# Attention scores whose low-part product contracts over 64 rows instead of 128, with keys copied by the vector engine instead of by transfers, and a regrouped projection and normalisation around them

## The chip, the cores and the metric

The kernel runs on one core of a Trainium2 chip. The core has a matrix engine (TensorE, PE in the profile, whose weight loads are listed apart as PEld), a vector engine (DVE), an activation engine (ACT), a general engine (POOL) and SyncE (SP), whose queue issues most transfers. The metric is the device time of one execution in microseconds (us). Before the change the median of three runs is 1168.81 us (1167.73 to 1170.11).

## The reference

Two decoder layers over 512 tokens of width 1024, in float32. Layer 0 mixes eight "a" heads (dilated sliding windows, merged by their softmax denominators) with eight "b" heads (window of 128, two key heads for eight query heads, a learned sink per head). Layer 1 has sixteen "c" heads of causal attention with a cumulative forget gate. Each layer ends in a squared-ReLU MLP of width 4096. Cut to what matters here:

```python
q = rms_norm(q.reshape(B, S, heads, 64), q_gain)      # over the 64 of a head
k = rms_norm(k.reshape(B, S, heads, 64), k_gain)
s = q @ k.T * 64 ** -0.5 + bias                        # bias: window and distance, or the forget gate
p = softmax(s)                                         # a: one sum over three windows; b: with a sink
y = p @ v
x = x + concat(y) @ w_out
x = x + square(relu(rms_norm(x) @ w_up)) @ w_down
```

## The kernel before, in words

**Arithmetic.** Float32 operands are used as two parts, a high part (the value rounded to the engine's fast float type) and a low part (value minus high part). A dense product is three matmuls: high by high, high by low, low by high (L163, L166, L167 in `mm3`; L230 to L232 in `project`). So nearly every operand is split, by a copy that makes the high part (`whi`, on ACT or POOL) and a subtraction that makes the low part (`wlo`, on DVE or POOL).

**Stages.** Start and first projection; layer 0 attention, up to about 235 us; its MLP, up to about 600 us; layer 1 attention, up to about 835 us; its MLP. In an attention stage two streams of work are woven into each other: dense matmuls (projections of the next heads, then the output projection) and the heads that are ready. `run` draws from the two generators by a ratio: `n_att` attention steps against `n_dense` units of dense work, with a lead. A step ends at each `yield`. A scheduler then orders each engine's instructions by priority, lower first, and by its own estimate of when operands are ready.

**One pair of heads.** `norm_heads` takes a projection out of four PSUM banks (copies L246), squares it (L248, ACT, out of PSUM), sums over 64 columns (L249), makes the inverse root on DVE (L252 and L127 to L133) and multiplies it in (L259: two of the four row tiles on DVE, two on POOL, by `NORM`). `prep_q` and `prep_k` transpose 128 columns, that is two heads, into a PSUM bank (`qkT`, L266). For head h, `prep_q` puts q's high part on the head's own 64 partitions (L276, ACT) and q's low part on the other 64 (L277, DVE). `prep_k` puts k's high part in block 0 and its low part in block 1 of a tile, both on the head's own 64 partitions (L158 ACT, L159 DVE), and a transfer copies both blocks to the other 64 partitions (L289, on SP's queue, 26 in all).

**Scores and softmax.** For each of four query tiles i, two matmuls make the scores (L324, L325): the stationary operand is the 128-partition column of q, high over low; the moving operand is block 0, then block 1 of k. Both contract over all 128 partitions, so that the two products carry all four part products. A "c" head adds a mask matmul (L327). A DVE instruction adds the bias and takes the row extreme (L338), ACT takes the exponential and its sum (L341), DVE the reciprocal (L344, one per tile i), and POOL (ACT for i = 3) scales the tile (L349, L346).

**Values.** For each key tile c, PE transposes the probabilities into a PSUM bank (L361); ACT and DVE split it (L373, L374); then eight matmuls per head make the output (L381), which is put together on ACT and DVE (L384, L385). The values of a head are made in the steps of the next head's scores.

Of the kernel before, what the change touches and what calls it, by code (L numbers as in the profile page):

```python
# [9 lines left out]
F32 = mybir.dt.float32  # L10
F32R = mybir.dt.float32r
# [26 lines left out]
NORM = 'vgvg'  # L38
PSC = 'ggga'
GRAIN = 4  # L40
STARTPIN = 4
# [30 lines left out]
def trunk(ctx, tc, x, g_mix, g_mlp, w_in_even, a_q_gain, a_k_gain, b_q_gain, b_k_gain, b_sinks,  # L72
# [45 lines left out]
    ecol = consts.tile([P, NT], F32, name="ecol")  # L118

# [71 lines left out]
    def layer_attention(li, hT, w_in, w_out, stats=None):  # L191


        with ExitStack() as c2:
# [9 lines left out]
            nc.gpsimd.memset(p3[:, :, 256:384].bitcast(F32), 0.0)  # L204
# [34 lines left out]
            def norm_heads(outs, nh, sq_tag="sq", sq_bufs=1 + li):  # L239
# [10 lines left out]
                v = small.tile([P, NT, 8], F32, tag="ssv", name="ssv")  # L250
                for t in range(NT):
                    nc.vector.tensor_scalar(v[:, t, :nh], ss[:, t, :nh], 1.0 / HD, ecol[:, t:t + 1],  # L252
                                            op0=OP.mult, op1=OP.add)
                rs = small.tile([P, NT, 8], F32, tag="rs", name="rs")
                rsqrt_small(rs[:, :, :nh], v[:, :, :nh])
                for t in range(NT):
                    q = qk[t // 2][:, t % 2, :w].rearrange("p (h d) -> p h d", d=HD)
                    eng = nc.gpsimd if NORM[t] == "g" else nc.vector
                    eng.tensor_mul(q, q, rs[:, t, :nh].unsqueeze(2).to_broadcast([P, nh, HD]))  # L259
                return qk  # L260
# [8 lines left out]
            def prep_q(qk, off):  # L269

                pt = head_T(qk, off)
                q = ap.tile([P, 2, 512], F32R, tag="Q", bufs=2, name="Q")
                for h in range(2):
# [3 lines left out]
                    nc.vector.tensor_sub(q[r2, h], pt[r], q[r, h].bitcast(F32))  # L277
                return q

            def prep_k(qk, off, g):  # L280
# [3 lines left out]
                for h in range(2):  # L284
                    k = ap.tile([P, 2, 512], F32R, tag="K", bufs=3, name="K")
# [15 lines left out]
            def scores(q, k, j, kind, h, pr):  # L301
# [11 lines left out]
                rden = small.tile([P, NT], F32, tag="rden", name="rden")  # L313
                for i in range(NT):
# [9 lines left out]
                    nc.tensor.matmul(s[:, :n], qs, k[:, 0, k0:k0 + n], start=True, stop=False)  # L324
                    nc.tensor.matmul(s[:, :n], qs, k[:, 1, k0:k0 + n], start=False, stop=kind != "c")  # L325
# [18 lines left out]
                    nc.vector.reciprocal(rden[:, i:i + 1], den[:, i:i + 1])  # L344
                    if PSC[i] == "a":
                        nc.scalar.activation(p[:, :nv], p[:, :nv], AF.Copy, scale=rden[:, i:i + 1])  # L346
                    else:
                        eng = nc.gpsimd if PSC[i] == "g" else nc.vector
                        eng.tensor_scalar(p[:, :nv], p[:, :nv], rden[:, i:i + 1], 1.0, op0=OP.mult, op1=OP.mult)  # L349
                    yield  # L350

            def values(pr, kind, V, vs, yf, j):

                pts = []
# [890 lines left out]
```

## Time and profile before

| what | us or share |
|---|---|
| median of three runs | 1168.81 |
| the profiled execution, its own time | 1168.43 |
| its span in the trace | 1166.7 |
| PE busy, of the span | 98% |
| DVE, ACT, POOL busy | 75%, 55%, 17% |
| layer 0 attention, from 45 to 235 us | 190 |
| layer 1 attention, from 600 to 835 us | 235 |

A page of the profile gives each engine's busy time and share. Matmuls are pipelined: each one is listed with its whole latency, so that the records of PE overlap, and what a matmul costs in a full stream is the distance from its start to the start of the next one, not its duration. A weight load (PEld) normally starts while the matmul before it still runs. "Idle before" is time of an engine without work, and the name behind it is what the profile holds for its releaser: this is inferred from the time of a semaphore event, and can be wrong.

### The profile page before, as it was taken

What the parts mean: (1) busy time and instruction counts of PE and PEld (TensorE: products, weight loads), DVE (VectorE), ACT (ScalarE), POOL (GpSimd) and SP (SyncE); (2) the same over time, 40 slices, a digit from 0 to 9 for tenths busy, and PEclk for the clock granted to TensorE, in tenths of its full rate; (3) what the DMA queues carried; (4) which work ended last, traced back from release to release, by engine and by line L of the source; (5) the groups of instructions that cost most, each with busy time, mean ns of one, the idle gap of its engine ahead of it and who ended that gap; (6) DMA issues with size and microseconds to landing.
All of it is one profiled execution on the core that took longest, in us unless ns stands there. A gap on an engine that the chain in (4) does not pass through costs nothing.

```text
span 1166.7 us, 17503 instructions
## 1 busy us (share of the span) xinstructions
PE 1146.8 (98%) x6256; PEld 982.5 (84%) x6256; DVE 880.7 (75%) x1877; ACT 647.1 (55%) x1349; POOL 202.4 (17%) x296
## 2 busy tenths in 40 slices
PE   8999989999999999999999999999999999999998
PEld 7987877888988988988887888888888888888887
DVE  7878999968858857855647877788858759669676
ACT  6555867556545545444235675656756455465452
POOL 1345444200000000000255445332100000000000
PEclk9999999999999999999999999999999999999999
DMA  7522014242333333333443333343430721623403
GB/s 253 163 76 89 19 57 146 70 126 78 104 108 91 91 108 91 106 111 110 146 128 109 107 84 109 107 118 113 163 105 4 235 87 55 198 73 109 147 33 109
DMA packets 100655, 126.57 MB, mean 108 GB/s; under 512 B 6184, under 2 KB 79944, under 8 KB 100568
## 3 DMA queue, kind: packets, MB, share of 16 engines
q1 hardware_dynamic: 99384, 121.23, 34.3%
q10 hardware_dynamic: 608, 2.13, 0.5%
q0 software_dynamic: 576, 2.10, 0.4%
q8 instruction: 49, 0.80, 0.3%
q14 instruction: 38, 0.31, 0.1%
HBM read 112.29 MB, written 6.32 MB: 102 GB/s over the span
## 4 chain that ended last, share of the span: by engine, by line
PE 85%; DVE 8%; DMA 2%; POOL 1%; issue 1%; ACT 1%; SPq 0%; ACTq 0%; POOLq 0%; DVEq 0%
PE up L163 10%; PE up L167 10%; PE up L166 10%; PE pj L230 5%; PE pj L232 5%; PE pj L231 5%; PE O L381 3%; PE PT L361 2%; PE Y L1021 2%; PE Y L1019 2%; PE Y L1022 2%; PE op L167 2%; PE op L163 2%; PE op L166 2%; PE Y L1068 1%; PE S L324 1%
## 5 line engine op out<-in xcount | busy, mean ns | idle before, releaser
L163 PE MATMUL up<-xin,whi 128*128 128x512 f32 x512 | 200.5, 392 | 0.0
L167 PE MATMUL up<-xin,whi 128*128 128x512 f32 x512 | 199.3, 389 | 0.0
L166 PE MATMUL up<-xin,wlo 128*128 128x512 f32 x512 | 199.2, 389 | 0.0
L768 ACT CAST whi<-wraw 128x512 fp32r<-128x512 f32 x228 | 139.2, 619 | 105.0 <-PE up L167 47.7
L769 DVE TENSOR_TENSOR wlo<-wraw,whi 128x512 fp32r<-128x512 f32 x228 | 151.7, 686 | 50.8 <-ACT whi L768 50.5
L167 PEld LDWEIGHTS up<-xin,whi 128*128 128x128 f32 x512 | 96.1, 188 | 20.1
L166 PEld LDWEIGHTS up<-xin,wlo 128*128 128x128 f32 x512 | 96.2, 188 | 19.8 <-issue 0.2
L163 PEld LDWEIGHTS up<-xin,whi 128*128 128x128 f32 x512 | 96.1, 188 | 19.8 <-issue 0.2
L341 ACT ACTIVATE P<-P,negm 128x128 f32<-128x128 f32 (+5 forms) x128 | 69.5, 544 | 51.7 <-DVE negm L338 47.9
L950 ACT ACTIVATE u<-up 128x512 f32<-128x512 f32 x64 | 38.3, 599 | 90.9 <-PE up L167 90.8
L230 PE MATMUL pj<-whi,hn 128*128 128x512 f32 (+2 forms) x256 | 88.7, 346 | 0.0
L232 PE MATMUL pj<-whi,hn 128*128 128x512 f32 (+2 forms) x256 | 86.9, 339 | 0.0
L231 PE MATMUL pj<-wlo,hn 128*128 128x512 f32 (+2 forms) x256 | 86.8, 339 | 0.0
L151 POOL TENSOR_SCALAR whi<-wraw 128x512 fp32r<-128x512 f32 x88 | 60.5, 689 | 143.0 <-PE pj L232 121.8
L789 DVE TENSOR_TENSOR t<-u 128x256 f32<-128x256 f32 x56 | 23.2, 424 | 62.8 <-ACT u L1093 61.0
L154 POOL TENSOR_TENSOR wlo<-wraw,whi 128x512 fp32r<-128x512 f32 x48 | 64.4, 1346 | 20.7 <-ACT whi L149 17.9
L230 PE MATMUL pj<-whi,h 128*128 128x512 f32 (+1 forms) x192 | 66.5, 353 | 0.7 <-DVE v L159 0.7
L232 PE MATMUL pj<-whi,h 128*128 128x512 f32 (+1 forms) x192 | 65.5, 343 | 0.0
L231 PE MATMUL pj<-wlo,h 128*128 128x512 f32 (+1 forms) x192 | 65.5, 341 | 0.0
L349 POOL TENSOR_SCALAR P<-P,rden 128x256 f32<-128x256 f32 (+2 forms) x96 | 47.7, 500 | 90.8 <-DVE rden L344 90.0
L154 DVE TENSOR_TENSOR wlo<-wraw,whi 128x512 fp32r<-128x512 f32 (+1 forms) x72 | 49.9, 700 | 17.7 <-POOL whi L151 14.5
L373 ACT CAST PT<-PT 128x256 fp32r<-128x256 f32 (+3 forms) x128 | 49.5, 405 | 19.4 <-PE PT L361 18.5
(229 smaller groups left out, 3054.4 us busy)
## 6 DMA issues: line engine op xcount, KB each, us to landing
wraw<-in_w_up SPq DMA_DIRECT2D x64, 512.0 KB, 3.8
wraw<-in_w_down SPq DMA_DIRECT2D x56, 512.0 KB, 4.2
wraw<-in_w_in_odd SPq DMA_DIRECT2D x36, 256.0 KB, 3.3
mraw<-in_w_down SPq DMA_DIRECT2D x16, 512.0 KB, 4.4
K<-K SPq DMA_DIRECT2D x26, 256.0 KB
wraw<-in_w_in_even SPq DMA_DIRECT2D x10, 512.0 KB, 4.0
wraw<-in_w_in_even SPq DMA_DIRECT2D x16, 256.0 KB, 4.5
xl<-xsp SPq DMA_DIRECT2D x8, 512.0 KB
```

Of the source, the lines that this page charges most:

```text
L151: nc.gpsimd.tensor_scalar(dst_h, src, 1.0, 1.0, op0=OP.mult, op1=OP.mult)
L154: in_order((nc.gpsimd if lo == "pool" else nc.vector).tensor_sub(dst_l, src, dst_h.bitcast(F32)))
L163: m = nc.tensor.matmul(o, wh, xh, start=start, stop=False, skip_group_check=more)
L166: nc.tensor.matmul(o, wl, xh, start=False, stop=False, skip_group_check=more)
L167: nc.tensor.matmul(o, wh, xl, start=False, stop=stop, skip_group_check=more)
L230: nc.tensor.matmul(o, xh, hi[:, :n], start=k == 0, stop=False)
L231: nc.tensor.matmul(o, xh, lo[:, :n], start=False, stop=False)
L232: nc.tensor.matmul(o, xl, hi[:, :n], start=False, stop=k == DC - 1)
L341: nc.scalar.activation(p[:, :ne], p[:, :ne], AF.Exp, scale=-1.0, bias=negm[:, i:i + 1], accum_out=den[:, i:i + 1])
L373: nc.scalar.copy(dst[:, 0], pt[:, :n])
L768: sca(nc.scalar.copy(dst_h, src))
L769: late.append(lambda: vec(nc.vector.tensor_sub(dst_l, src, dst_h.bitcast(F32))))
```

## The change

What it does:

- **Scores.** q's high part is now written to both halves of the partitions (one more ACT copy per head and pair), and q's low part goes to a third block, each head on its own 64 partitions. k has its high part on the head's own 64 partitions and its low part on the other 64, in one block. The first matmul contracts over 128 partitions as before. The second has q's low part as stationary operand and k's high part as moving operand, over the 64 partitions of one head only. The product of the two low parts is left out.
- **Keys.** The 26 transfers of k are gone: DVE writes the low part straight to the other half. For the "b" heads, whose keys serve query heads of both halves, two ACT copies (`KH`) put the high part there as well.
- **Projection of the "b" heads.** 256 columns (keys and values) and then 512 (queries) become 384 twice, the second time with the values.
- **Normalisation.** All four copies out of PSUM come first; squares are taken from the copy, and all that follows gets a priority lower by 100. The four small L252 instructions become one, and all four multiplications are on DVE.
- **Softmax scale.** The reciprocals of i = 0, 1, 2 are one instruction, behind i = 2.
- **Values.** Key tiles 3 and 2 share one bank and one split (for "b" heads, 0 and 1 as well): three or two splits instead of four. A head thereby has one step less ("b": two less); the ratios given to `run` stay.

```diff
             def norm_heads(outs, nh):
...
                 for t in range(NT):
-                    q = qk[t // 2][:, t % 2, :w]
-                    nc.scalar.copy(q, outs[t][:, :w])
-                    sq = ap.tile([P, 512], F32, tag=sq_tag, bufs=sq_bufs, name="sq")
-                    nc.scalar.activation(sq[:, :w], outs[t][:, :w], AF.Square)
-                    nc.vector.reduce_sum(ss[:, t, :nh], sq[:, :w].rearrange("p (h d) -> p h d", d=HD), axis=AX.X)
...
-                    eng = nc.gpsimd if NORM[t] == "g" else nc.vector
-                    eng.tensor_mul(q, q, rs[:, t, :nh].unsqueeze(2).to_broadcast([P, nh, HD]))
+                    nc.scalar.copy(qk[t // 2][:, t % 2, :w], outs[t][:, :w])
+                with later(LATER):
+                    for t in range(NT):
+                        q = qk[t // 2][:, t % 2, :w]
+                        sq = ap.tile([P, 512], F32, tag="sq", bufs=1 + li, name="sq")
+                        nc.scalar.activation(sq[:, :w], q, AF.Square)
...
+                        nc.vector.tensor_mul(q, q, rs[:, t, :nh].unsqueeze(2).to_broadcast([P, nh, HD]))
...
-                q = ap.tile([P, 2, 512], F32R, tag="Q", bufs=2, name="Q")
+                q = ap.tile([P, 3, 512], F32R, tag="Q", bufs=2, name="Q")
                 for h in range(2):
                     r = slice(h * HD, (h + 1) * HD)
                     r2 = slice((1 - h) * HD, (2 - h) * HD)
                     nc.scalar.copy(q[r, h], pt[r])
-                    nc.vector.tensor_sub(q[r2, h], pt[r], q[r, h].bitcast(F32))
+                    nc.vector.tensor_sub(q[r, 2], pt[r], q[r, h].bitcast(F32))
+                    nc.scalar.copy(q[r2, h], pt[r])
...
-                    scale_split(k[r, 0], k[r, 1], pt[r], g[r])
-                    nc.sync.dma_start(k[r2].bitcast(F32), k[r].bitcast(F32))
-                    ks.append(k)
+                    in_order(nc.scalar.activation(k[r], pt[r], AF.Copy, scale=g[r]))
+                    in_order(nc.vector.scalar_tensor_tensor(k[r2], pt[r], g[r], k[r].bitcast(F32), op0=OP.mult, op1=OP.subtract))
+                    his = [k, k]
+                    if both:
+                        his[1 - h] = ap.tile([P, 512], F32R, tag="K", bufs=4, name="KH")
+                        nc.scalar.copy(his[1 - h][r2], k[r].bitcast(F32))
+                    ks.append((k, his))
...
-                    nc.tensor.matmul(s[:, :n], qs, k[:, 0, k0:k0 + n], start=True, stop=False)
-                    nc.tensor.matmul(s[:, :n], qs, k[:, 1, k0:k0 + n], start=False, stop=kind != "c")
+                    nc.tensor.matmul(s[:, :n], qs, k[0][:, k0:k0 + n], start=True, stop=False)
+                    r = slice(j * HD, (j + 1) * HD)
+                    nc.tensor.matmul(s[:, :n], q[r, 2, i * P:(i + 1) * P], k[1][j][r, k0:k0 + n], start=False,
+                                     stop=kind != "c")
...
-                for c in range(NT):
+                for cs in (((0, 1), (3, 2)) if kind == "b" else ((0,), (1,), (3, 2))):
...
-                    return project([(2048, 2304)], use, PAT_START)
+                    return project([(1792, 2048), (2176, 2304)], use)
```

In the order of the instructions two places matter. The first is PE in layer 0, where the first pair of "a" heads gets its scores. `S<-K,Q` are the score matmuls, `pj` the dense projection woven around them. Before (L324 is the first of a pair, L325 the second):

```order
L231 MATMUL pj_615<-wlo,h_5_281 128x256
L232 MATMUL pj_615<-whi,h_5_281 128x256
L324 MATMUL S<-K,Q 128x256
L325 MATMUL S<-K,Q 128x256
L324 MATMUL S<-K,Q 128x256
L325 MATMUL S<-K,Q 128x256
L324 MATMUL S<-K,Q 128x384
L325 MATMUL S<-K,Q 128x384
```

And now (L338 is the first of a pair, L340 the second, which contracts over 64 partitions):

```order
L237 MATMUL pj_615<-whi,h_1_170 128x384
L338 MATMUL S<-K,Q 128x256
L340 MATMUL S<-K,Q 128x256
L238 MATMUL pj_615<-wlo,h_1_170 128x384
L239 MATMUL pj_615<-whi,h_1_170 128x384
L338 MATMUL S<-K,Q 128x256
L340 MATMUL S<-K,Q 128x256
L237 MATMUL pj_612<-whi,h_2_208 128x384
```

Every L340 stands between two matmuls that contract over 128 partitions, here and in all of the program (128 of them). The scores also moved forward: ten dense matmuls of 384 columns lie between the transposes of this pair and its first score, where 42 of 256 columns lay before.

The second place is ACT at the same pair: the casts that make q's and k's parts, up to the first exponential. Before:

```order
L276 CAST Q<-qkT 64x512
L158 ACTIVATE K<-qkT,gg 64x512
L276 CAST Q<-qkT 64x512
L158 ACTIVATE K<-qkT,gg 64x512
L341 ACTIVATE P,den<-P,negm 128x128
```

And now (L283 is q's high part on the own half, L285 on the other half):

```order
L283 CAST Q<-qkT 64x512
L297 ACTIVATE K<-qkT,gg 64x512
L285 CAST Q<-qkT 64x512
L283 CAST Q<-qkT 64x512
L297 ACTIVATE K<-qkT,gg 64x512
L285 CAST Q<-qkT 64x512
L357 ACTIVATE P,den<-P,negm 128x128
```

Six casts instead of four stand ahead of the exponentials, and the first score waits for the first three.

More of the change, by code (lines that the diff above doesn't have):

```diff
@@ L1 @@
-from contextlib import ExitStack
+from contextlib import ExitStack, contextmanager
 import numpy as np
@@ L343, in scores @@
                     pr.append(p)
[L344 to L349, printed above, removed]
+                    ps_.append(p[:, :nv])
@@ new lines, in scores @@
+                    if i >= 2:
+                        i0 = 0 if i == 2 else 3
+                        nc.vector.reciprocal(rden[:, i0:i + 1], den[:, i0:i + 1])
+                        for n in range(i0, i + 1):
+                            if PSC[n] == "a":
+                                nc.scalar.activation(ps_[n], ps_[n], AF.Copy, scale=rden[:, n:n + 1])
+                            else:
+                                nc.gpsimd.tensor_scalar(ps_[n], ps_[n], rden[:, n:n + 1], 1.0, op0=OP.mult, op1=OP.mult)
```

86 lines of the change are left out of this document (48 added, 38 removed).

## Prediction

> **What bounds the kernel now.** I read the page first, then the waits of PE, then the stages, then single matmuls in the timeline.
>
> ```profile
> PE 1146.8 (98%) x6256; PEld 982.5 (84%) x6256; DVE 880.7 (75%) x1877; ACT 647.1 (55%) x1349; POOL 202.4 (17%) x296
> ```
>
> And the busy times of the four attention stretches, PE first, then PEld, DVE, ACT, POOL:
>
> ```profile
> 45.00:110.00 65.00, 62.12 (x370) 53.47 (x369) 50.61 (x139) 34.15 (x87) 34.86 (x48) 1.00 0.31 90
> 110.00:160.00 50.00, 48.09 (x325) 41.84 (x324) 46.35 (x158) 39.56 (x118) 23.63 (x59) 1.00 0.13 43
> 160.00:235.00 75.00, 72.12 (x377) 59.59 (x376) 70.35 (x161) 49.42 (x115) 23.42 (x31) 1.00 0.32 93
> 600.00:835.00 235.00, 231.87 (x1371) 197.33 (x1370) 184.14 (x475) 144.02 (x335) 96.30 (x125) 1.00 0.39 111
> ```
>
> PE is the bound everywhere: it lacks 2.9, 1.9, 2.9 and 3.1 us, 10.8 us in all. Since each record of a matmul reaches past its start-to-start distance, the true loss is somewhat larger; I take up to 14 us as all that a change of waits can bring. From 110 to 235 us DVE is at 93% (46.35 of 50, 70.35 of 75), so there it is the second limit. What PE waits for, with total, times and longest:
>
> ```profile
> PE S L324 <- DMA K<-K: 2.6, 3, 1.1
> PE S L324 <- DVE yf L385: 1.8, 2, 1.6
> PE S L324 <- DVE Q L277: 1.8, 2, 1.5
> PE qkT L266 <- DVE qk L259: 1.3, 2, 0.9
> PE O L381 <- DVE PT L374: 0.8, 2, 0.6
> PE PT L361 <- DVE negm L338: 0.8, 2, 0.6
> PE pj L230 <- DVE v L159: 0.7, 1, 0.7
> ```
>
> The transfers of k cost 2.6 us of PE time, DVE in six places 7.2 us. So little can be won; what the change does to the matmuls themselves weighs more.
>
> **The matmuls.** Their number is the same, 6247 in the program. The projection moves 96 matmuls of 512 and 96 of 256 columns to 192 of 384. In a full stream they start this far apart:
>
> ```profile
> 35.01 0.39 PE L231 MATMUL pj<-wlo,h 128*128 128x512 f32 x1
> 35.24 0.39 PE L232 MATMUL pj<-whi,h 128*128 128x512 f32 x1
> ```
>
> ```profile
> 626.66 0.34 PE L325 MATMUL S<-K,Q 128*128 128x384 f32 x1
> 626.84 0.23 PE L327 MATMUL S<-maskb,identb 128*128 128x128 bf16 x1
> ```
>
> ```profile
> 640.51 0.28 PE L232 MATMUL pj<-whi,hn 128*128 128x256 f32 x1
> 640.63 1.04 PE L266 MATMUL qkT<-ident,qk 128*128 128x128 f32 x8
> 641.42 0.36 PE L230 MATMUL pj<-whi,hn 128*128 128x256 f32 x1
> 641.62 0.28 PE L231 MATMUL pj<-wlo,hn 128*128 128x256 f32 x1
> ```
>
> That is 0.23 us for 512 columns, 0.18 for 384, 0.12 for 256: 96 x (0.23 + 0.12) = 34 us against 192 x 0.18 = 35 us. Nothing within a microsecond. The last four rows are also a control: eight transposes over 128 rows plus one matmul of 256 take 640.63 to 641.62, 0.99 us, that is 8 x 0.11 + 0.12 within the rounding. Going to transposes and back costs nothing.
>
> The second score matmul is another matter: 128 times it contracts over 64 rows between matmuls that contract over 128. The trace has one such excursion in a dense stream, the transpose of 22 rows of gains right behind the matmul of 35.24 above (the number ahead of the star is the rows, the one behind it the columns of the stationary operand):
>
> ```profile
> 35.56 0.24 PE L623 MATMUL pg<-ident,rows 22*128 22x22 f32 x1
> 35.72 0.38 PE L230 MATMUL pj<-whi,h 128*128 128x256 f32 x1
> 35.95 0.28 PE L231 MATMUL pj<-wlo,h 128*128 128x256 f32 x1
> ```
>
> Its weight load and the next one, and the semaphores that its line waited for:
>
> ```profile
> 35.55 0.13 PEld L623 LDWEIGHTS pg<-ident,rows 22*128 22x128 f32 x1 [0.35 <-ACT whi L149]
> 35.72 0.19 PEld L230 LDWEIGHTS pj<-whi,h 128*128 128x128 f32 x1
> ```
>
> ```profile
> L623 PEldq EVENT_SEMAPHORE  x5: 51/51/51, 2.7 to 31.7; - x5
> ```
>
> The weight load for the 22 rows should have run beside the 512-column matmul and let the next one start at 35.24 + 0.23 = 35.47. It started at 35.55, 0.09 late, and only then loaded. The next load, of full rows, came at 35.72 instead of beside the short matmul, and the matmul on it could stream only when it was in: 35.72 to 35.95 is 0.23 where 0.12 is the rule. From 35.24 to 35.95 it took 0.71 us; with a transpose of full rows it would be 0.23 + 0.11 + 0.12 = 0.46. The excursion cost 0.25 us. The named releaser (the cast of a weight tile) is a coincidence of time: the transpose reads rows whose semaphores had been seen by 31.7 us (last line) and no weight tile. So PE empties itself when the number of rows changes, and weight loads are not hidden on either side.
>
> The Trainium skill says so of tiling modes: "TensorEngine Tiling (Array Packing)", section Key Properties, has it that a change of mode, not of the tile alone, drains the engine. By that rule every one of the 128 matmuls pays twice, as in the sum below; a reading by which a half-height matmul is just a smaller one gives nothing. The trace agrees for the 22 rows and disagrees for a narrow stationary operand, which is the second rival.
>
> For a score matmul I put the pieces together: 0.09 late, 0.11 for the load that is no longer hidden, its own 256 columns as before, then a rest of 0.02 to 0.09 (0.17 between the two loads above, less 0.11 of loading and 0.03 of streaming; or as late as at the entry), and 0.11 for the next load. That is 0.33 to 0.40; the bare figure of 0.25 is the lower bound, since the short transpose's own slot was itself a weight load's. 128 times: 32 us below, 42 by 0.33, 51 above. I take 42, the low end of the built price, since half of the exits go to the short bf16 mask load. It is all on PE, the bound, and nothing hides it.
>
> **The rest, by engine.** Prices:
>
> ```profile
> L276 ACT CAST Q<-qkT 64x512 fp32r<-64x512 f32 x32 | 18.6, 582 | 28.8 <-PE qkT L266 20.4 <-DVE Q L277 8.2
> L159 DVE SCALAR_TENSOR_TENSOR K<-qkT,gg,K 64x512 fp32r<-64x512 f32 x26 | 19.5, 749 | 0.7
> L373 ACT CAST PT<-PT 128x256 fp32r<-128x256 f32 x48 | 17.4, 371 | 11.1 <-PE PT L361 10.8
> L373 ACT CAST PT<-PT 128x384 fp32r<-128x384 f32 x24 | 11.4, 477 | 2.4 <-PE PT L361 2.3
> L373 ACT CAST PT<-PT 128x128 fp32r<-128x128 f32 x32 | 8.5, 264 | 2.3 <-PE PT L361 2.3
> L344 DVE RECIPROCAL rden<-den 128x1 f32<-128x1 f32 x128 | 19.9, 159 | 7.0 <-ACT P L341 5.2
> L252 DVE TENSOR_SCALAR ssv<-ss,ecol 128x8 f32<-128x8 f32 x28 | 9.6, 362 | 0.2
> L259 DVE TENSOR_TENSOR qk<-qk,rs x16: 294/1526/1553, 44.2 to 759.9; 128x512 f32<-128x512 f32 x14, 128x128 f32<-128x128 f32 x2
> L259 POOL TENSOR_TENSOR qk<-qk,rs x16: 443/1488/1544, 44.3 to 759.4; 128x512 f32<-128x512 f32 x14, 128x128 f32<-128x128 f32 x2
> 705.62 0.69 DVE L259 TENSOR_TENSOR qk<-qk,rs 128x512 f32<-128x512 f32 x1
> 54.71 3.34 DMA K<-K
> ```
>
> ACT gets 34 more casts of 0.58 (20 us). Of the PT casts it loses 48 of 256 and 32 of 128 columns (25.9 us) and gets 32 more of 384 (15.3 us) and 8 of 512 (at most 0.6 each, by the step from 256 to 384 once more): 6 us less. DVE loses 64 reciprocals of 0.159 (10 us), some 8 us of L252 and about as much as ACT, 6 us, of PT subtractions. The multiplications L259 take 1.5 us on either engine while both work on them, and 0.69 where DVE's comes first; four in a row on DVE are 2.8 us, as long as POOL's two, so that move costs DVE about 4 us (24 x 0.69 and some smaller ones for 16) and the chain nothing. DVE ends 20 us lighter, half of it in layer 0 where it is at 93%. With that, and with PE slower by a tenth, I expect 5 of the 7.2 us of DVE waits to go.
>
> The transfer of 3.34 us leaves the chain from transposes to first score, and with it 2.6 us of waits. But the scores now stand ten matmuls of 384 columns, 1.8 us, behind the transposes, and the chain ahead of them is two casts and a scaling on ACT plus a DVE pass of 0.75: about 2 us where ACT is free. At 12 pairs that make keys I allow 0.3 us each, 4 us of new waits (bounds 0 and 8). Behind the waiting score PE's queue stands still, dense matmuls too. SP's queue loses 26 transfers and gets ten more weight loads (384 columns come as 256 and 128); PE waits for no weights in the list above, so nothing. The step ratios, unchanged with fewer steps, end the heads earlier and leave dense matmuls behind, which costs a bound PE nothing.
>
> Sum, from the profiled execution's 1168.4: + 42 - 2.6 - 5 + 4 = **1206 us**, and that execution is as good as the median of 1168.8. Ends: 1168.4 + 32 - 10 = 1190, and 1168.4 + 51 - 5 + 8 = 1222.
>
> **Rivals.** First, the cheaper switch: only the exit counts, the load that isn't hidden, 0.11 x 128 = 14 us, since the score's 64-row load may still find room beside the first score matmul: 1168.4 + 14 - 4 = 1179, range 1172 to 1188. For it: only one clean sample stands behind the entry's 0.09. Against: that sample.
>
> Second, and on the other side, a half-height matmul costs no switch at all; then only waits change, 1168.4 - 2.6 - 5 + 4 = 1165, range 1157 to 1169. For it stand the transposes of 16 columns:
>
> ```profile
> 585.11 0.29 PE L232 MATMUL pj<-whi,hn 128*128 128x272 f32 x1
> 585.23 0.49 PE L725 MATMUL pz<-ident,fz 128*16 128x128 f32 x3
> 585.48 0.48 PE L230 MATMUL pj<-whi,hn 128*128 128x512 f32 x1
> ```
>
> Up to the matmul behind them it takes 585.48 - 585.11 = 0.37 us, 0.12 + 2 x 0.11 + 0.03, no loss at either end. Against it: those keep 128 rows, and the 22 rows don't. It decides for a gain if a switch costs under 4 / 128 = 0.03 us.
>
> Third, no switch cost but the new casts late: ACT's 20 us more make the 16 first scores wait 0.5 us and more, and the time is back at about 1171.
>
> **Numbers.** The forecast has 0.66, the cheaper switch 0.13, no switch cost 0.17, late casts 0.04. Forecast alone: 1190 to 1222. The range for 8 in 10 takes in the cheaper switch and part of the free one: 1161 to 1220. About 0.2%, 2.3 us, is what a measurement here can tell from no change: faster 0.15 (most of the free switch), same 0.04, slower 0.81.
>
> **What would show it.** If right, L340's weight load starts about 0.2 us after L338 starts at 256 columns and the matmul behind L340 some 0.5 us after L340's load, instead of 0.12 apart; both attention stretches are longer by 15 to 25 us each, the MLPs the same; waits for K<-K are gone; L259 on DVE is near 0.69 us. Wrong if L338 and L340 start 0.12 us apart and the next matmul 0.12 later; then the time is below 1170. If the stretches grow but by idle time in front of L338, it is the casts and not the switch.

## The result, and the profile after

The changed kernel takes **1201.82 us** (median of four runs, 1201.20 to 1202.85), against 1168.88 us for the kernel before: a ratio of 1.0286, 95% interval 1.0273 to 1.0298. It is slower by 33 us. The forecast was 1206 in a range of 1161 to 1220; the first rival (1179), the second (1165) and the third (1171) did not come about. The sum came near with its terms taken together in one kernel; taken out one at a time, as in the experiments, the terms have other sizes, and the small ones another sign.

Busy time of the engines in the profiled execution after (its own time is 1201.2, its span 1199.4):

```profile
PE 1185.6 (99%) x6256; PEld 993.4 (83%) x6256; DVE 873.3 (73%) x1769; ACT 672.8 (56%) x1347; POOL 180.5 (15%) x280
```

PE has as many instructions as before and is busy 38.8 us longer. ACT gained 26 us, DVE lost 7. To see where, I cut both spans at the same points of the program: start, attention of layer 0, its MLP, attention of layer 1, its MLP. (Cut so, layer 0's attention before ends at 229.4 us, and layer 1's starts at 572.3 and not at about 600.) The columns are the window, its length, and the busy time of PE, PEld, DVE, ACT and POOL with instructions in brackets, then the granted clock, the DMA share and GB/s. Before:

```profile
45.00:229.40 184.40, 176.74 (x1041) 150.28 (x1041) 161.71 (x447) 118.56 (x311) 81.91 (x136) 1.00 0.27 81
229.40:572.30 342.90, 342.39 (x1983) 303.49 (x1983) 245.94 (x454) 175.77 (x318) 0.31 (x1) 1.00 0.34 102
572.30:829.50 257.20, 254.07 (x1518) 217.86 (x1517) 194.12 (x501) 146.28 (x339) 112.96 (x142) 1.00 0.41 119
829.50:1166.70 337.20, 333.08 (x1489) 275.60 (x1487) 243.69 (x393) 177.38 (x322) 0.00 (x0) 1.00 0.33 105
```

After:

```profile
45.00:243.40 198.40, 196.08 (x1037) 158.56 (x1037) 155.87 (x391) 131.51 (x307) 71.64 (x130) 1.00 0.21 66
243.40:586.20 342.80, 342.29 (x1983) 303.40 (x1982) 245.80 (x454) 175.74 (x318) 0.31 (x1) 1.00 0.34 102
586.20:862.20 276.00, 273.67 (x1517) 220.62 (x1517) 192.89 (x449) 158.84 (x339) 104.10 (x134) 1.00 0.31 96
862.20:1199.40 337.20, 333.13 (x1489) 275.61 (x1488) 243.69 (x393) 177.36 (x322) 0.00 (x0) 1.00 0.33 105
```

The MLPs are the same to a tenth. Layer 0's attention is 14.0 us longer (198.4 against 184.4), layer 1's 18.8. The second number against the first shows how: PE's idle time fell from 7.7 to 2.3 us in layer 0 and from 3.1 to 2.3 in layer 1, 6.1 in all, while its busy time grew by 19.3 and 19.6, with as many matmuls at a clock of 1.00 in both. So PE waits less for others and takes longer for as many matmuls.

Where, the timeline of PE in a dense stretch shows (start, duration, then line and operands; a duration holds the latency, so starts are to be compared):

```profile
52.68 0.34 PE L239 MATMUL pj<-whi,h 128*128 128x384 f32 x1
52.86 0.28 PE L338 MATMUL S<-K,Q 128*128 128x256 f32 x1
53.06 0.38 PE L340 MATMUL S<-K,Q 64*128 64x256 f32 x1
53.38 0.45 PE L237 MATMUL pj<-whi,h 128*128 128x384 f32 x1
53.66 0.34 PE L238 MATMUL pj<-wlo,h 128*128 128x384 f32 x1
53.84 0.33 PE L239 MATMUL pj<-whi,h 128*128 128x384 f32 x1
```

And the weight loads in the same stretch:

```profile
53.06 0.18 PEld L340 LDWEIGHTS S<-K,Q 64*128 64x128 f32 x1 [0.19 <-issue]
53.37 0.19 PEld L237 LDWEIGHTS pj<-whi,h 128*128 128x128 f32 x1
53.48 0.19 PEld L238 LDWEIGHTS pj<-wlo,h 128*128 128x128 f32 x1
```

From L338 to L340 it is 0.20 to 0.21 us for 256 columns where 0.12 is the rule: +0.09. From L340 to L237, 0.31 instead of 0.12: +0.19. From L237 to L238, 0.28 instead of 0.18: +0.10, since the load of L237 did not start until 53.37, 0.31 us behind the start of L340; the next load (53.48) is 0.11 behind it. In all 0.38 to 0.39 us for one matmul over 64 rows. The load of L340, at 53.06, shows the same at the entry: it starts 0.20 us after L338, which takes 0.12 us in a full stream, and "issue" says that it waited for nothing that the profile names.

Half of the pairs, those of the "c" heads, have the short mask matmul (L343) behind them. There the third piece is missing:

```profile
636.50 0.36 PE L338 MATMUL S<-K,Q 128*128 128x256 f32 x1
636.79 0.38 PE L340 MATMUL S<-K,Q 64*128 64x256 f32 x1
637.11 0.23 PE L343 MATMUL S<-maskb,identb 128*128 128x128 bf16 x1
637.14 0.48 PE L237 MATMUL pj<-whi,hn 128*128 128x512 f32 x1
```

From L340 to L343 it is 0.32 us, the same exit, but the next matmul starts 0.04 us (0.039) behind L343, and 0.039 is also the median behind scores of 256 columns in the kernel with zeros below, which has no switch. So only entry and exit are paid there.

PE's waits after (what waited, for whom; total, times, longest):

```profile
PE O L404 <- ACT PT L397: 1.6, 2, 0.9
PE O L404 <- DVE PT L398: 1.1, 2, 0.7
PE S L338 <- ACT Q L285: 0.8, 2, 0.6
...
PE S L338 <- DVE K L298: 0.4, 2, 0.2
PE qkT L273 <- DVE qk L266: 0.2, 1, 0.2
```

The waits for the transfers of k (2.6 us) are gone, and so are those for `yf`, Q's low part, `negm` and v. New are 1.2 us before first scores, for the casts and k's low part, and 1.6 in the output for a cast of PT.

### The profile page after: what moved, and what is told of

It is laid out like the page before. It is cut to its first block, busy times and chain, and to the rows that moved or that the text cites. A ratio compares the mean times of both kernels' runs of the same rounds, so it can differ in the third digit from the quotient of the medians.

```text
span 1199.4 us, 17313 instructions
## 1 busy us (share of the span) xinstructions
PE 1185.6 (99%) x6256; PEld 993.4 (83%) x6256; DVE 873.3 (73%) x1769; ACT 672.8 (56%) x1347; POOL 180.5 (15%) x280
## 4 chain that ended last, share of the span: by engine, by line
PE 92%; DVE 4%; ACT 2%; POOL 1%; DMA 0%; issue 0%; SPq 0%; DVEq 0%; POOLq 0%; ACTq 0%
PE up L174 10%; PE up L170 10%; PE up L173 10%; PE pj L237 6%; PE pj L238 6%; PE pj L239 5%; PE S L340 3%; PE O L404 3%; PE PT L384 3%; PE op L173 2%; PE op L170 2%; PE op L174 2%; PE S L338 2%; PE Y L1048 2%; PE Y L1045 2%; PE Y L1047 2%
## 5 line engine op out<-in xcount | busy, mean ns | idle before, releaser
L158 POOL TENSOR_SCALAR whi<-wraw 128x512 fp32r<-128x512 f32 (+1 forms) x88 | 56.4, 643 | 231.6 <-PE pj L239 194.8
L237 PE MATMUL pj<-whi,hn 128*128 128x512 f32 (+2 forms) x256 | 88.7, 347 | 0.0
L238 PE MATMUL pj<-wlo,hn 128*128 128x512 f32 (+2 forms) x256 | 87.0, 340 | 0.0
L357 ACT ACTIVATE P<-P,negm 128x128 f32<-128x128 f32 (+5 forms) x128 | 69.4, 542 | 30.5 <-DVE negm L354 26.8
L161 POOL TENSOR_TENSOR wlo<-wraw,whi 128x512 fp32r<-128x512 f32 (+1 forms) x48 | 64.7, 1347 | 29.3 <-ACT whi L156 21.8
L161 DVE TENSOR_TENSOR wlo<-wraw,whi 128x512 fp32r<-128x512 f32 (+2 forms) x76 | 50.8, 675 | 23.6 <-POOL whi L158 19.5
L237 PE MATMUL pj<-whi,h 128*128 128x512 f32 (+2 forms) x192 | 66.5, 352 | 0.0
L238 PE MATMUL pj<-wlo,h 128*128 128x512 f32 (+2 forms) x192 | 66.0, 344 | 0.0
L239 PE MATMUL pj<-whi,h 128*128 128x512 f32 (+2 forms) x192 | 65.6, 342 | 0.0
L354 DVE CUSTOM_DVE_ANT_0 P<-S,bias 128x128 f32<-128x128 f32 (+1 forms) x96 | 45.8, 486 | 27.3 <-PE S L343 17.8
L397 ACT CAST PT<-PT 128x384 fp32r<-128x384 f32 (+1 forms) x88 | 45.0, 516 | 35.1 <-PE PT L384 34.7
```

The costliest lines, as they stand in the source:

```text
L158: nc.gpsimd.tensor_scalar(dst_h, src, 1.0, 1.0, op0=OP.mult, op1=OP.mult)
L161: in_order((nc.gpsimd if lo == "pool" else nc.vector).tensor_sub(dst_l, src, dst_h.bitcast(F32)))
L237: nc.tensor.matmul(o, xh, hi[:, :n], start=k == 0, stop=False)
L238: nc.tensor.matmul(o, xh, lo[:, :n], start=False, stop=False)
L239: nc.tensor.matmul(o, xl, hi[:, :n], start=False, stop=k == DC - 1)
L354: nc.vector.tensor_tensor_reduce(out=p[:, :nv], in0=s[:, :nv], in1=b, op0=OP.add, op1=OP.min, scale=-0.125, scalar=nsink[:, h:h + 1] if ki ...
```

## The experiments

All were timed beside the kernel before on the same chip, 1167.7 to 1168.4 us there; ratios are to it. Not all were on one chip, so a difference between two of them can be off by about the 1 us by which the kernel before differs. The theory: each stretch of 64 rows in PE's stream costs it 0.3 to 0.4 us, and that is what the change loses. The main rival: the loss is in the new chains (casts, keys, later normalisation), and PE only looks slow.

### The low product over all rows, with zeros

The same product without a change of row height: q's low parts lie in two tiles whose other half is zero, and the second score matmul contracts over all 128 rows. What is computed is what the changed kernel computes; two small ACT copies for the "b" heads and four settings to zero on POOL are added.

```diff
+            ql = [ap.tile([P, 512], F32R, tag=f"QL{h}", name=f"QL{h}") for h in range(2)]
+            for h in range(2):
+                nc.gpsimd.memset(ql[h][(1 - h) * HD:(2 - h) * HD].bitcast(F32), 0.0)
...
-                    nc.tensor.matmul(s[:, :n], q[r, 2, i * P:(i + 1) * P], k[1][j][r, k0:k0 + n], start=False,
+                    nc.tensor.matmul(s[:, :n], ql[j][:, i * P:(i + 1) * P], k[1][j][:, k0:k0 + n], start=False,
```

> The changed kernel, but the second score matmul contracts over all 128 rows again: q's low part lies in a tile of its own per head, with zeros on the other head's 64 rows, so that the result is the same; two more ACT copies fill the other half of KH. All else is as changed. Switch theory: the 128 changes of row height go, about 40 us of PE time with them (0.28 to 0.38 us each), and some 0 to 6 us of waits come back: 1162 to 1168 us, so no slower than the kernel before, and L340 starts 0.12 us behind L338 at 256 columns. Rival (the loss comes from the regrouped projection, late normalisation, fewer steps or the added ACT casts): it stays at 1190 us or more.

Measured 1175.05 us, ratio 1.0060 (1.0048 to 1.0073). Filling half of the rows with zeros saves 26.8 us (25.6 if each kernel is compared with the kernel before beside it), so the switch is the main loss. In the timeline the three pieces are gone:

```profile
54.03 0.28 PE L342 MATMUL S<-K,Q 128*128 128x256 f32 x1
54.14 0.28 PE L343 MATMUL S<-K,QL 128*128 128x256 f32 x1
54.26 0.34 PE L240 MATMUL pj<-whi,h 128*128 128x384 f32 x1
```

The starts are 0.11 and 0.12 apart. q's low part has one buffer here where Q has two, but that is not felt: in all of these kernels it is written 2.6 us or more after the last score of the pair ahead. But the rest was expected to leave a gain, and it costs 7 us:

```profile
PE O L407 <- ACT PT L400: 2.9, 2, 1.7
...
PE O L407 <- DVE PT L401: 2.2, 4, 0.9
...
PE PT L387 <- POOL P L371: 1.0, 3, 0.6
```

PE waits 5.1 us in the output for the splits of PT, where before it waited 1.0. In the changed kernel itself, with its slower PE, these waits are 2.7.

### The score part alone, and the rest alone

Two kernels that divide the change: before with the new q, k and score matmuls only, and the changed kernel with q, k and scores as before.

```diff
 # the score part alone, in the kernel before
-                    nc.tensor.matmul(s[:, :n], qs, k[:, 1, k0:k0 + n], start=False, stop=kind != "c")
+                    nc.tensor.matmul(s[:, :n], q[r, 2, i * P:(i + 1) * P], k[1][j][r, k0:k0 + n], start=False,
+                                     stop=kind != "c")
...
 # the rest alone, in the changed kernel
+                    scale_split(k[r, 0], k[r, 1], pt[r], g[r])
+                    nc.sync.dma_start(k[r2].bitcast(F32), k[r].bitcast(F32))
```

> The kernel before, with the score part of the change alone: q's high part on both halves, keys' low part on the other half without transfers, the second score matmul over 64 rows. Switch theory: 1168.9 + 40 less up to 8 us of waits: 1201 to 1209 us. Rival (the rest of the change makes the loss): at most 1175 us.

> The changed kernel with the score part as before (keys duplicated by transfers, both score matmuls over 128 rows), so everything else of the change alone. Switch theory: the rest costs nothing and may gain: 1160 to 1169 us. Rival: 1190 us or more.

The score part alone: 1200.96 us, ratio 1.0280 (1.0266 to 1.0294). The rest alone: 1171.9 us, ratio 1.0040 (1.0026 to 1.0054). The first is almost the whole loss. The second refutes the reading that the rest gains: it costs 4 us. The two do not add up (33.2 + 4.2 = 37, measured 32.9 for both): behind a PE that is slower by the switch, the rest costs nothing that these runs can tell (ratios of 1.0286 with it and 1.0280 without, with intervals that overlap).

### The score part with zeros

The score part alone, without a change of row height: the same two edits as above, in the kernel before.

> The kernel before with the score part alone, and its second score matmul over 128 rows with zeros under q's low part, so without a change of height. Switch theory: the run of the score part alone (1201.0) less some 40 us of switches, with 4 to 8 us of waits coming back: 1165 to 1169 us. If the casts and keys of the score part cost something themselves: 1172 us or more. If to have no transfers of k gains what PE waited for them (2.6 us): 1163 to 1166.

Measured 1172.84 us, ratio 1.0041 (1.0029 to 1.0054). Against 1200.96 with 64 rows, the switch is worth 28.1 us here, 26 to 27 in the whole change: 0.20 to 0.22 us net for each of the 128. And the score part, without any switch, costs 5 us instead of gaining 2.6. About 1 us of it belongs to these kernels with zeros alone: both lose 1.1 us at the small transposes of layer 1 (`pz`), where the kernels without the zeros lose 0.1. PE's waits:

```profile
PE O L392 <- DVE PT L385: 2.1, 3, 1.3
...
PE S L334 <- DVE K L294: 1.7, 2, 1.1
...
PE qkT L269 <- POOL qk L262: 1.1, 2, 0.5
```

The wait for the transfer of k has gone to its neighbour: the first score now waits 1.7 us for DVE's part of k, where before it waited 2.6 us for the transfer behind it. The rest is spread over small waits; layer 1's attention is 4.1 us longer than before, layer 0's the same.

### The casts alone

The kernel before with 32 ACT casts more, at the place where the change has its own. Each writes into the half of Q that the low part then overwrites, so the chain to the first score is one cast longer.

```diff
                     nc.scalar.copy(q[r, h], pt[r])
+                    nc.scalar.copy(q[r2, h], pt[r])
                     nc.vector.tensor_sub(q[r2, h], pt[r], q[r, h].bitcast(F32))
```

> The kernel before, with one more ScalarE cast of 64 x 512 for each half of each pair of query heads (32 in all, 18.6 us of ScalarE by the 0.582 us of such a cast), which writes into the half of Q that the low part then overwrites, so that the chain from the transposes to the first score is one cast longer. The 32 casts stand where the changed kernel has its own; nothing else of the change is in. Theory that these casts are the 5 us which the score part costs without any change of row height: 1171 to 1175. Rival, that ScalarE at 55% takes them for nothing and the 5 us come from the K scaling or from the order: 1167 to 1169.

Measured 1167.22 us, ratio 0.9993 (0.9984 to 1.0001). The casts cost nothing here, neither as ACT's time nor as one more step of a chain that ends in k's transfer. That speaks against them as the source of the 5 us of the score part; that they cost nothing without the transfers as well isn't shown. What is left of that part is k's scaling and low part in the place of the transfers and the scheduler's order that comes with it; these were not separated.

### The price of a change of height, by itself

The kernel before, with nothing of the change. In the MLP's up projection PE never waits, and every fourth low product there (128 matmuls of 512 columns) contracts over 64 of its 128 rows. The other half of these products is left out.

```diff
-        nc.tensor.matmul(o, wl, xh, start=False, stop=False, skip_group_check=more)
+        nc.tensor.matmul(o, wl[:rows], xh[:rows], start=False, stop=False, skip_group_check=more)
...
-                        "p" in PINS and k == 0 and pinned[0])
+                        "p" in PINS and k == 0 and pinned[0], rows=HD if k == 1 else P)
```

> The kernel before, all attention untouched. In the MLPs' up projections every fourth low-part product (weights' low part by the high input; 128 in all, 512 columns) contracts over 64 of its 128 rows, leaving the other half of that product out. Number and width of matmuls are the same, and there PE works in a full stream without waits, so this prices the switch by itself. Switch theory, with the entry 0.09, exit 0.19 and late load 0.10 that the changed kernel's trace shows: 0.38 x 128 = 49 us, so 1214 to 1221 us. Rival (a change of height costs only next to transposes, bf16 masks or waits, as in attention): 1167 to 1172 us.

Measured 1219.93 us, ratio 1.0442 (1.0428 to 1.0456): 52.2 us more, 0.41 each, for matmuls that do half of the work. Both MLPs are 25.7 us longer, the attention stretches as before within 0.7. The timeline of PE, and the weight loads:

```profile
437.42 0.39 PE L163 MATMUL up<-xin,whi 128*128 128x512 f32 x1
437.74 0.50 PE L166 MATMUL up<-xin,wlo 64*128 64x512 f32 x1
438.17 0.50 PE L167 MATMUL up<-xin,whi 128*128 128x512 f32 x1
438.50 0.39 PE L163 MATMUL up<-xin,whi 128*128 128x512 f32 x1
438.73 0.39 PE L166 MATMUL up<-xin,wlo 128*128 128x512 f32 x1
```

```profile
437.74 0.18 PEld L166 LDWEIGHTS up<-xin,wlo 64*128 64x128 f32 x1 [0.35 <-issue]
438.17 0.19 PEld L167 LDWEIGHTS up<-xin,whi 128*128 128x128 f32 x1 [0.25 <-issue]
438.27 0.19 PEld L163 LDWEIGHTS up<-xin,whi 128*128 128x128 f32 x1
```

In the full stream the starts lie 0.23 apart. Here 0.32 (entry, +0.09), 0.43 (exit, +0.20) and 0.33 (behind the load that was not hidden, +0.10). These are the pieces that the changed kernel shows around its scores. They are the same for 512 columns as for 256.

### By change or by matmul

The same 128 stretches, with two products over 64 rows, one right behind the other, in each: 256 matmuls of half height, as many changes of height. The other half of 256 products is left out.

```diff
+                for k, r in ((1, slice(0, HD)), (2, slice(0, HD))):
+                    nc.tensor.matmul(o, lo[r, k], x[k][r, 0], start=False, stop=False)
```

> As in the run on the up projections, but two neighbouring low-part products of every four contract over rows 0 to 63 alone and stand next to each other: 256 half-height matmuls in 128 pairs, so twice the half-height matmuls and the same number of changes of height (the other halves of those products are left out). If the price is per change of height: like that run, 1217 to 1223 us. If it is per half-height matmul (its weight load never hidden): 1260 to 1275 us.

Measured 1222.28 us, ratio 1.0462 (1.0446 to 1.0478). Twice the half-height matmuls at the same number of changes cost 2 us more, not 52. The price is per change.

If that is so, the changed kernel can get some of it back. Here its score matmuls of two neighbouring query tiles are issued together, both over 128 rows and then both over 64:

```diff
+                        for low in range(2):
+                            for d in range(2):
...
+                                if low:
+                                    nc.tensor.matmul(ss_[d][:, :n], q[r, 2, cols], k[1][j][r, k0:k0 + n], start=False,
+                                                     stop=kind != "c")
+                                else:
+                                    nc.tensor.matmul(ss_[d][:, :n], q[:, j, cols], k[0][:, k0:k0 + n], start=True, stop=False)
```

> The changed kernel, with the score matmuls of two neighbouring query tiles issued together: both products over 128 rows, then both over 64 rows. The matmuls are the same 256; the stretches of 64 rows in PE's order fall from 128 to 77, 51 fewer. If the price is per change of row height: 51 x 0.21 (net, from the comparison with zero rows) to 51 x 0.31 (in place, from the trace) = 11 to 16 us less, 1186 to 1191. If it is per matmul of 64 rows, 1201 to 1203. If the second PSUM bank that is now taken early makes PE wait, some of the gain is lost: 1192 to 1200.

Measured 1189.31 us, ratio 1.0177 (1.0163 to 1.0191): 12.5 us less than the changed kernel for 51 stretches fewer, 0.245 us each, between the two prices. Some of the gain is lost again: PE waits 4.6 us in the output for a split of PT, where in the changed kernel it waited 2.7. One group in the timeline (x2: two matmuls in one row, the start is the first one's):

```profile
56.56 0.40 PE L341 MATMUL S<-K,Q 128*128 128x256 f32 x2
56.88 0.50 PE L338 MATMUL S<-K,Q 64*128 64x256 f32 x2
57.31 0.45 PE L237 MATMUL pj<-whi,h 128*128 128x384 f32 x1
57.60 0.34 PE L238 MATMUL pj<-wlo,h 128*128 128x384 f32 x1
```

0.32 for two full products (+0.08), 0.43 for two over 64 rows (+0.19), 0.29 for the matmul behind (+0.11): 0.38 for the pair, as much as one product cost above.

A pair of products on opposite halves of the rows, one behind the other, wasn't tried.

### The width instead of the height

The same 128 products of the up projection, with 64 of the 128 columns of the stationary operand and all rows (half of their outputs is left out).

```diff
-        nc.tensor.matmul(o, wl, xh, start=False, stop=False, skip_group_check=more)
+        nc.tensor.matmul(o[:rows], wl[:, :rows], xh, start=False, stop=False, skip_group_check=more)
```

> As in the run on the up projections, but the same 128 products keep all 128 rows and use 64 of the 128 columns of their stationary operand (they write half of the output's rows; the other half of those products is left out). If only a change of row height empties PE, as the transposes of 16 columns in the trace of before suggest: 1165 to 1170 us. If any change of the tile's shape does: 1210 us or more.

Measured 1170.73 us, ratio 1.0023 (1.0014 to 1.0032): 2.9 us for 128, 0.02 each (at most 0.03 by the interval). A matmul with a narrow stationary operand takes no longer than the others:

```profile
436.61 0.39 PE L163 MATMUL up<-xin,whi 128*128 128x512 f32 x1
436.83 0.40 PE L166 MATMUL up<-xin,wlo 128*64 128x512 f32 x1
437.07 0.39 PE L167 MATMUL up<-xin,whi 128*128 128x512 f32 x1
```

The starts are 0.22 to 0.24 apart, with the narrow one as without. The Trainium skill says in "TensorEngine Tiling (Array Packing)", section Key Properties, that changing the tiling mode drains the engine. For rows the runs agree (0.41 us for going and coming back). For 64 columns they show 0.02; no trace here tells whether the mode changes with them.

### What the rest loses by

The rest alone with `run`'s step numbers scaled to the fewer steps of a head:

```diff
-                run(att_a(0), 32, chain(qk_b(), qv_b()), 768, LEADS[0])
+                run(att_a(0), 29, chain(qk_b(), qv_b()), 768, LEADS[0])
...
-                    run(att_c(g), 36, chain(qk_c(g + 1), v_c(g + 1)), 768, LEADS[3 + g])
+                    run(att_c(g), 32, chain(qk_c(g + 1), v_c(g + 1)), 768, LEADS[3 + g])
```

> The run of everything but the score part (1171.9 us), with the step numbers given to the weaving of heads and dense work scaled to the fewer steps of a head (32, 86, 38, 36, 42 become 29, 68, 34, 32, 37). If the 4 us that the rest cost come from heads that run ahead of the dense work: back to 1166 to 1169 us. If they come from the later normalisation or the merged splits: 1170 to 1174 us.

Measured 1171.34 us, ratio 1.0026 (1.0014 to 1.0038), against 1.0040 (1.0026 to 1.0054) with the old numbers. The intervals overlap; it is not the ratios, or little of it.

The rest alone, with reciprocal and scaling tile by tile as before:

```diff
-                    if i >= 2:
-                        i0 = 0 if i == 2 else 3
-                        nc.vector.reciprocal(rden[:, i0:i + 1], den[:, i0:i + 1])
...
+                    nc.vector.reciprocal(rden[:, i:i + 1], den[:, i:i + 1])
```

> The rest of the change alone (scores and keys as before), but with the reciprocal and the scaling of each query tile by itself, as in the kernel before, in place of one reciprocal for tiles 0, 1 and 2 behind tile 2. With that grouping the rest alone took 1171.9 and PE waited 4.2 us in its transposes of the probabilities behind VectorE and 1.1 us behind GpSimd's scaling. If the grouping of the reciprocals is what the rest loses by, the gain of the small normalisation parts (4 us) shows: 1162 to 1167, and those waits are near the 0.8 us of before. If the loss is in the lower priority of the normalisation, in the projection of 384 columns twice or in the merged splits: 1170 to 1173.

Measured 1169.0 us, ratio 1.0014 (1.0004 to 1.0023): 2.9 us of the 4 are the grouped reciprocals and scalings. With them, PE's transposes of the probabilities (L376) waited:

```profile
PE PT L376 <- DVE negm L346: 4.2, 3, 1.9
...
PE PT L376 <- POOL P L360: 1.1, 2, 0.7
```

Without them (the same line is L373):

```profile
PE PT L373 <- DVE negm L346: 2.1, 2, 1.3
...
PE PT L373 <- POOL P L357: 1.4, 3, 1.0
```

The first wait is halved, both together fall from 5.3 to 3.5 us and not to the 0.8 of before, and the time lies between the two ranges expected, near the upper one. So the grouping is a part of the loss, not all.

Last, the kernel before with two small parts of the rest: all four multiplications of the normalisation on DVE, and one instruction for the four of L252.

```diff
-NORM = 'vgvg'
+NORM = 'vvvv'
...
-                for t in range(NT):
-                    nc.vector.tensor_scalar(v[:, t, :nh], ss[:, t, :nh], 1.0 / HD, ecol[:, t:t + 1],
-                                            op0=OP.mult, op1=OP.add)
+                nc.vector.scalar_tensor_tensor(v[:, :, :nh], ss[:, :, :nh], 1.0 / HD,
+                                               ecol.unsqueeze(2).to_broadcast([P, NT, nh]), op0=OP.mult, op1=OP.add)
```

> The kernel before, with only two small parts of the rest of the change: all four scaling multiplications L259 on VectorE, and one instruction in place of four for L252. If VectorE and GpSimd slow each other in L259 (1.5 us against 0.69 us in the rows of before) and VectorE at 93% is a limit in layer 0, the prediction's reading, 1163 to 1167. If VectorE's load costs PE nothing that is not already hidden, 1167 to 1170. If VectorE's four in a row come late for the transposes: 1170 to 1173.

Measured 1164.33 us, ratio 0.9963 (0.9950 to 0.9977): 4 us faster than the kernel before, and the fastest kernel of this study. Where DVE took 1.53 us beside POOL for a multiplication, it now takes:

```profile
L258 DVE TENSOR_TENSOR qk<-qk,rs x32: 278/682/1782, 42.6 to 755.1; 128x512 f32<-128x512 f32 x28, 128x128 f32<-128x128 f32 x4
```

0.68 in the median; six of the 32 still take 1.1 us or more. In the profiled executions layer 0's attention is 2.6 us shorter than before, layer 1's 3.1. Which of the two small parts brings it was not separated.

So the rest holds a gain of 4 us and a loss of 3 by the grouped reciprocals, and yet costs 4. If the parts add up, some 5 us are lost in what remains: the lower priority of the normalisation, 384 columns twice, and the merged splits of PT. That is a difference of runs, not a run of its own, and which of the three it is stays open.

## Why the prediction was right, and where it was not

**The mechanism and its price in place: right.** "PE empties itself when the number of rows changes, and weight loads are not hidden on either side" is what the timeline shows, with the pieces that were read from one transpose of 22 rows: entry +0.09, exit +0.19 to +0.20, next load +0.10 to +0.11. The built price was 0.33 to 0.40; the dense streams show 0.38 to 0.41. For all 128 pairs I took the distance from each start to the next, less the median distance of matmuls of that width. Around the pairs this sums to 47 us after and to 7.7 in the changed kernel with zeros: 39 us, 0.31 each, against the 42 of the sum. The low end was rightly taken, and for its reason: by the same count the 64 pairs with the mask behind them cost 0.27 each, the others 0.34.

**"It is all on PE, the bound, and nothing hides it": wrong.** The term of 42 us is 26 to 28 net, by two pairs of runs that differ in the rows and in little else (1201.82 against 1175.05, 1200.96 against 1172.84). PE was idle for 11.2 us in the attention stretches with zeros and for 4.7 with the switch:

```profile
45.00:230.30 185.30, 179.97 (x1050) 154.95 (x1050) 156.03 (x393) 131.99 (x310) 74.22 (x130) 1.00 0.23 70
573.20:836.40 263.20, 257.31 (x1518) 217.42 (x1517) 192.48 (x449) 157.54 (x339) 104.31 (x134) 1.00 0.33 100
```

(these are the two stretches of the kernel with zeros: 185.30 - 179.97 and 263.20 - 257.31). The count of starts shows the whole of it. Outside the pairs PE loses 32 us with zeros and 18 with the switch, so 13 or 14 of the 39 are time that it would have lost elsewhere: 3.9 at the transposes of the probabilities, 3.3 in the output, 2.6 at other score matmuls, the rest in small pieces. I read it so that a PE slowed at many places gives the other engines time.

**"- 2.6 - 5 + 4": right in sign in the kernel that has the switch, wrong without it.** The sum wrote these terms for a PE that is slower by a tenth. In that kernel the loss outside the pairs is 18 us against 26 before, 8 less, where the sum had 3.6 less; around the pairs it is 47 against 7, 40 more, where the sum had 42. Both differences go the same way and make the forecast's 1206 a little too high. But the terms are no prices of the parts. Without the switch the rest of the change measures +7.3 us (1175.05 against 1167.73), and the second rival, "no switch cost", which used the same terms for a PE that isn't slowed, would have been 1175, not 1165. The three terms one by one:

- **-2.6, the transfers of k.** Their waits are gone, but the chain behind them isn't: the first scores wait 1.7 us for DVE's part of k in the score part with zeros (0.4 in the whole change with zeros). A wait was taken off the sum without asking what was late next.
- **+4, the casts.** 0 by the run with the casts alone (0.9993), 1.2 us of waits before first scores in the trace after. The low bound was the better end.
- **-5, DVE's waits.** In the list of waits after, DVE's have fallen from 7.2 to 1.7 us, as forecast. But the reason that the prediction names first, 20 us less work on DVE, doesn't carry it: with zeros, at the same work, PE waits 4.3 us for DVE in the attention stretches, and 3.6 for ACT and 1.6 for POOL, where before it was 0.4 for both. So about half of the fall needs the slower PE, which the prediction names second, and the other half comes back at other engines. The durations of all DVE instructions sum to 19 less, but its busy time fell only by 7.4 (880.7 to 873.3), since many of the small ones lay beside others. And the waits are set by chains, not by the load: the grouped reciprocals put off the scaling of the first two tiles, and in the run of the rest alone PE waited 5.3 us at the transposes behind them, 3.5 without the grouping. The prediction counted these reciprocals as a gain in DVE time only.

So the change has two descriptions that both add up to the 33 us measured, within the 1 us between chips: 40 for the switch and 8 saved elsewhere, in place, or 7 for the rest and then 26 to 28 for the switch. The waits that the rest makes are those that the switch then hides.

**Slips in the working.** The 26 transfers are those of 13 pairs that make keys, not 12. The load at 35.55 is 0.08 behind 35.47, and 0.17 less 0.14 is 0.03, not 0.02. The sum as written is 1206.8. These move the forecast by 1 or 2 us. Of the signs that were named, the matmul behind L340 comes 0.31 us after L340's load and not 0.5, and layer 0's attention grew by 14.0 us, a little under the 15 to 25; layer 1's 18.8 lies inside.

**The multiplications on DVE: right in price.** 0.682 us in the median after, predicted near 0.69. All of them together take DVE 6.0 us more (18.4 to 24.4), predicted 4. What the prediction missed is that this is worth something alone: "the chain nothing" was too little, 4 us are to be had together with the merged L252.

**The step ratios and the MLPs: right.** Scaling the ratios is worth 0.6 us by the medians and 0.0014 by the ratios, with intervals that overlap, and both MLPs last as long as before.

**The rivals.** The cheaper switch (the exit alone) is refuted by the entry in every timeline shown and by the 0.41 of the MLP. The free switch is refuted for rows; the transposes of 16 columns that spoke for it agree with the run with 64 columns, which costs 0.02 each. Late casts are refuted by the trace after: PE's idle time in attention fell by 6.1 us, and the first scores wait 1.2 us in all for casts and k.

## What to carry to other kernels

Count, in PE's order, how often the number of rows of the stationary operand changes: on a bound PE each excursion to 64 rows cost 0.3 to 0.4 us in place here, more than the matmul itself, and 0.2 net where other waits then vanished. Other heights were not measured, but for one transpose of 22 rows. Fill the missing rows with zeros, or put the short matmuls next to each other in PE's order. When waits are taken off a sum, follow the chain to what is late next, and check the sign of the small terms with a run that has the change without its main mechanism: here the sum came near, and yet the rest, which it had as a gain of 4 us, costs 7 as soon as the main term is taken away.

## What the runs showed of the hardware that was not expected

- The price of a change in row height is per change and not per matmul (256 half-height matmuls in 128 pairs: 1222.28 us; 128 single ones: 1219.93), and the same at 256 and 512 columns. A stationary operand of 64 columns costs 0.02 us (1170.73 against 1167.81 for 128).
- Half the rows filled with zeros is faster than half the rows left out, by 26.8 us in this kernel.
- DVE's multiplication with an operand broadcast along the row takes 0.68 us in the median where all are on DVE and took 1.53 us while POOL made the other half of them: all four in a row on DVE are faster than two on each engine.
